# Gate and up projections of two SwiGLU blocks: another form of Strassen's seven products, with results made in place in PSUM

## The chip, the cores and the metric

The kernel runs on one core of a Trainium2 chip. The metric is the device time of one execution in microseconds (us). A core has five engines that run their own queues of instructions and wait for one another through semaphores: PE (TensorE, matrix products; its weight loads are shown as PEld), DVE (VectorE), ACT (ScalarE), POOL (GpSimd) and SP (SyncE, which issues most of the transfers). Matrix products write into PSUM, which has eight banks of 128 partitions by 512 float32 values; DVE and ACT can read and write it too.

## The reference, cut to what matters

One layer of a decoder, 1024 tokens of width 1024, in float32. A gated feed-forward block (SwiGLU, hidden width 2816) stands before and after a mixer of delta-rule and state-space heads:

```python
def swiglu(h, w_gate, w_up, w_down):
    a = jnp.einsum("bld,df->blf", h, w_gate)
    b = jnp.einsum("bld,df->blf", h, w_up)
    return jnp.einsum("blf,fd->bld", jax.nn.silu(a) * b, w_down)

x = x + 0.5 * swiglu(rms_norm(x, ffn1_norm[i]), ffn1_w_gate[i], ffn1_w_up[i], ffn1_w_down[i])
x = x + hybrid_mixer(rms_norm(x, mix_norm[i]), w_in[i], ...)
x = x + 0.5 * swiglu(rms_norm(x, ffn2_norm[i]), ffn2_w_gate[i], ffn2_w_up[i], ffn2_w_down[i])
```

## The kernel before

**Precision.** Each factor of a product is split into a high part, rounded to fp32r (ACT, the "cast" of L239), and the rest, also fp32r (DVE, L240). A product is three matrix products, high by high, high by low and low by high, added in one PSUM bank (L332, L333, L334 in `prod`).

**Strassen.** The gate and up projections are made by Strassen's form. The weights of one *item* are 256 columns of `w_gate` or of `w_up` and all 1024 rows: four blocks of 512 by 128, called a11, a12, a21, a22. The normalised and transposed tokens are four blocks of 512 by 512, two of them from the first 512 tokens (`x0`) and two from the last (`x1`). Seven products of sums of weight blocks by sums of token blocks, with sums of the products, give the four blocks c11, c12, c21, c22 of the result. A product is 12 matmuls (4 steps over the 512 rows, 3 parts each) of 512 columns; an item is 84 matmuls. There are 22 items in each feed-forward block (11 column groups, gate and up in turn): items 0 and 1 are written out, items 2 to 21 are a loop.

**Operands of the tokens.** `b_first` (L261) makes what needs only `x0`, `b_second` (L271) the rest: transposes on PE (L216, four of 128 by 128 into one bank with tag "sc"), scaling, sums and splits on ACT and DVE. This is done once in each block, before and while the first products run.

**Operands of the weights.** `a_load` brings an item's weights (1 MB) into one of two `wst` buffers. `a_ops` (L304) makes the sums (DVE, L315) and the splits for a group of up to four products, into one of two pairs of buffers `ah`, `al`. In the loop an item's next operands are made in two groups (`A_GROUPS`), called by `prep(0)` and `prep(1)`. `a_start` makes those of items 0 and 1 in the four groups of `A_START`.

**Results.** `open_bank` (L336) makes a product in a fresh bank and, where asked, copies it to SBUF (ACT, L341). In the loop products 3, 2 and 1 are copied so; 5, 4 and 7 are then added by PE to the same banks, 6 has the bank "oo". Six sums on DVE (L445, L446, L450, L451, L461, L464) put the four blocks together. For a gate item ACT takes the silu (L454, L455, L466, L467); for an up item DVE multiplies (L458, L459, L470, L471) and `hid_store` makes five sums (L490) and stores seven operands of the next product, the down projection, to DRAM.

**Order.** Each engine works through its own queue in order. The queues' orders are set when the program is built, by a planner that goes by the written order as priority and takes, at each point of its own estimate of time, the first instruction that it holds for ready. `tc.issue_after` adds an edge to that. A tile gets its buffer when the earlier tile of its tag is done with it. PSUM's banks have the tags "pj" (3), "mx" (2), "sc" (2) and "oo" (1).

**The stages in time.** Gate and up of the first block run from about 17 to 453 us, its down projection (L552 to L554) to about 667, the mixer with its input and output projections (L121 to L123) to 1657, gate and up of the second block to about 2088, its down projection to the end.

Of the kernel before, what the change touches and what calls it, by code (L numbers as in the profile page):

```python
# [21 lines left out]
P = 128  # L22
# [22 lines left out]
def kernel(  # L45
# [196 lines left out]
    def split(hi, lo, src):  # L242
# [7 lines left out]
    B_TAGS = {2: (ha, "h0", "h1"), 4: (ha, "h2", "h3"), 7: (ha, "h4", "h5"), 6: (ha, "h6", "h7"),  # L250
              3: (None, "b0", "b1"), 1: (None, "b2", "b3"), 5: (None, "b4", "b5")}
# [9 lines left out]
    def b_first(pool, x0, wcol, H, r11):  # L261

        for k in range(4):
            A.mul(out=r11[:, k], in_=transposed(x0, k), mul=wcol[:, k:k + 1])
            split(b_op(H, 2)[0][:, k], b_op(H, 2)[1][:, k], r11[:, k])
            t = pool.tile([P, 512], F32, name="bs4", tag="q")
            V.scalar_tensor_tensor(out=t, in0=transposed(x0, k + 4), scalar=wcol[:, k + 4:k + 5],
                                   in1=r11[:, k], op0=ALU.mult, op1=ALU.subtract)
            split(b_op(H, 4)[0][:, k], b_op(H, 4)[1][:, k], t)

    def b_second(pool, x0, x1, wcol, H, r11, r22, between):  # L271

        def operand(m, k, f):
            t = pool.tile([P, 512], F32, name="bs", tag="q")
            f(t)
            return split2(b_op(H, m)[0][:, k], b_op(H, m)[1][:, k], t)

        def scaled(pt, kx, other, op):
            return lambda t: V.scalar_tensor_tensor(out=t, in0=pt, scalar=wcol[:, kx:kx + 1], in1=other,
                                                    op0=ALU.mult, op1=op)  # L280

        for k in range(4):
            A.mul(out=r22[:, k], in_=transposed(x1, k + 4), mul=wcol[:, k + 4:k + 5])
            p12 = transposed(x1, k)
            operand(3, k, scaled(p12, k, r22[:, k], ALU.subtract))
            operand(6, k, scaled(p12, k, r11[:, k], ALU.add))
        between(0)
        for k in range(4):
            split(b_op(H, 5)[0][:, k], b_op(H, 5)[1][:, k], r22[:, k])
        for k in range(4):  # L290
            operand(7, k, scaled(transposed(x0, k + 4), k + 4, r22[:, k], ALU.add))
        between(1)
        for k in range(4):
            last = operand(1, k, lambda t: V.tensor_tensor(out=t, in0=r11[:, k], in1=r22[:, k], op=ALU.add))
        return last

    A_GROUPS = ((3, 2, 1, 5), (4, 7, 6))
# [6 lines left out]
    def a_ops(pool, *prods):  # L304

        hi = wp.tile([P, 4, 4, P], F32R, name="ah", tag="whi")
        lo = wp.tile([P, 4, 4, P], F32R, name="al", tag="wlo")
        for i, (raw, m, ops) in enumerate(prods):
            a11, a12 = raw[:, 0:4, 0:P], raw[:, 4:8, 0:P]
            a21, a22 = raw[:, 0:4, P:2 * P], raw[:, 4:8, P:2 * P]  # L310
            v = {3: a11, 4: a22, 2: (a21, a22, ALU.add), 1: (a11, a22, ALU.add), 5: (a11, a12, ALU.add),
                 7: (a12, a22, ALU.subtract), 6: (a21, a11, ALU.subtract)}[m]
            if isinstance(v, tuple):
                t = pool.tile([P, 4, P], F32, name="as", tag="q")
                V.tensor_tensor(out=t, in0=v[0], in1=v[1], op=v[2])  # L315
                v = t
# [5 lines left out]
    A_START = (((0, 2), (0, 4), (1, 2), (1, 4)), ((0, 3), (1, 3), (0, 6), (1, 6)),  # L322
               ((0, 5), (1, 5), (0, 7), (1, 7)), ((0, 1), (1, 1)))
# [4 lines left out]
    def prod(H, bank, ops, m, first):  # L328
# [6 lines left out]

    def open_bank(H, st, c, m, t, tag=None):  # L336

        bank = st[c] = psum(tag or {"c12": "pj", "c21": "mx", "c11": "pj", "c22": "oo"}[c])
        prod(H, bank, st, m, True)
        if t is not None:  # L340
            A.copy(out=t, in_=bank)  # L341
            st[f"m{m}"] = t

    def first_products(pool, H, ops):

        for st in ops:
            open_bank(H, st, "c21", 2, pool.tile([P, 512], F32, name="m2f"))
            prod(H, st["c21"], st, 4, False)
        for st in ops:
            open_bank(H, st, "c12", 3, pool.tile([P, 512], F32, name="m3", tag="q"))  # L350

    def gate_up_all(pool, H, w_gate, w_up, scr, raws, ops, last, work, tail):

        todo = [(p, w) for p in range(NF2) for w in (w_gate, w_up)]
        loads = todo[4:]

# [3 lines left out]
        def next_load():  # L360
            raws.pop(0)
            if loads:
                pn, wn = loads.pop(0)
                raws.append(a_load(wn, pn))


        for c, m in (("c22", 6), ("c11", 7)):
            for j, st in enumerate(ops):
                open_bank(H, st, c, m, wtile(True, f"m{m}"), ("pj", "oo")[j])
            if m == 6:  # L370
                for st in ops:
                    prod(H, st["c12"], st, 5, False)
        s12, s21 = (wtile(True, name) for name in ("sg12", "sg21"))
        nxt = [{}]

        def gated(o, bank, j):
            if j == 0:
                return A.activation(out=o, in_=bank, func=AF.Silu)
            return V.tensor_tensor(out=o, in0=bank, in1=o, op=ALU.mult)


        with tc.issue_after(last[0].ins), tc.issue_after(last[1].ins):
            for j, st in enumerate(ops):
# [1103 lines left out]
```

## Time and profile before

| | us |
|---|---|
| median of 3 runs | 2309.02 (2308.48 to 2310.09) |
| the profiled execution | 2309.97 |
| its span, first to last instruction | 2308.2 |
| PE busy | 2272.5 (98%) |
| DVE busy | 1725.1 (75%) |
| ACT busy | 1088.8 (47%) |
| TensorE clock granted, mean | 0.998 |

An engine's busy time is the time in which at least one of its instructions was in work. Instructions overlap in the engine's pipeline: a row's duration of one instruction is longer than the step from one to the next. A matmul's end is modelled, so PE's busy share says little of its rate; the step from one start to the next does.

### The profile page before, as it was taken

How to read it: one execution, taken by the hardware profiler on the slowest of the kernel's cores; microseconds unless marked ns; L12 is line 12 of the kernel's file. 1: busy time of each engine (PE TensorE's matmuls, PEld its weight loads, DVE VectorE, ACT ScalarE, POOL GpSimd, SP SyncE). 2: the span in 40 equal slices, each digit the busy share in tenths (PEclk: the TensorE clock that was granted, in tenths of full speed). 3: DMA queues.
4: the chain of work that ended last, by engine and by line, in shares of the span. 5: the costliest groups of instructions: out<-in, count | busy, mean ns of one | idle time of the engine just before them, and what ended most of it. 6: DMA issues, size and time to landing. Idle time of an engine off the chain costs nothing.

```text
span 2308.2 us, 31393 instructions
## 1 busy us (share of the span) xinstructions
PE 2272.5 (98%) x11750; PEld 1858.9 (81%) x11750; DVE 1725.1 (75%) x3349; ACT 1088.8 (47%) x1884; POOL 53.1 (2%) x125
## 2 busy tenths in 40 slices
PE   7999999999999999999999999999999999999998
PEld 5788888888878888878788888788778888888886
DVE  7977776767765675668777888878688777766787
ACT  7433333343367785863555555332543333334344
POOL 0000000000000100000000000000000000000000
PEclk9999999999999999999999999999999999999999
DMA  3333332573652332232333322335223333329446
GB/s 111 127 114 102 105 109 97 178 278 128 222 179 78 92 92 81 67 85 74 83 101 83 82 74 73 104 110 193 79 84 117 109 103 105 109 88 354 139 154 214
DMA packets 231438, 281.42 MB, mean 122 GB/s; under 512 B 57449, under 2 KB 164045, under 8 KB 230261
## 3 DMA queue, kind: packets, MB, share of 16 engines
q1 hardware_dynamic: 231028, 279.31, 37.5%
q8 instruction: 92, 1.51, 0.3%
q14 instruction: 62, 0.50, 0.1%
q0 software_dynamic: 256, 0.10, 0.0%
HBM read 211.59 MB, written 67.77 MB: 121 GB/s over the span
## 4 chain that ended last, share of the span: by engine, by line
PE 87%; DVE 6%; ACT 3%; DMA 2%; issue 1%; SPq 0%; POOL 0%; DVEq 0%; ACTq 0%
PE ps_pj L121 9%; PE ps_pj L123 9%; PE ps_pj L122 9%; PE ps_pj L334 6%; PE ps_pj L332 6%; PE ps_pj L333 6%; PE ps_mx L332 3%; PE ps_mx L334 3%; PE ps_mx L333 3%; PE ps_pj L553 2%; PE ps_pj L554 2%; PE ps_pj L552 2%; PE ps_oo L333 2%; PE ps_oo L332 2%; PE ps_oo L334 2%; PE ps_sc L552 1%
## 5 line engine op out<-in xcount | busy, mean ns | idle before, releaser
L121 PE MATMUL ps_pj<-hhi,whi 128*128 128x512 f32 x832 | 334.3, 402 | 0.4 <-ACT gsb L826 0.4
L123 PE MATMUL ps_pj<-hhi,wlo 128*128 128x512 f32 x832 | 334.5, 402 | 0.0
L122 PE MATMUL ps_pj<-hlo,whi 128*128 128x512 f32 x832 | 331.8, 399 | 0.0
L334 PE MATMUL ps_pj<-bh,al 128*128 128x512 f32 x688 | 267.9, 389 | 0.0
L333 PE MATMUL ps_pj<-bl,ah 128*128 128x512 f32 x688 | 267.8, 389 | 0.0
L332 PE MATMUL ps_pj<-bh,ah 128*128 128x512 f32 x688 | 267.6, 390 | 0.0
L123 PEld LDWEIGHTS ps_pj<-hhi,wlo 128*128 128x128 f32 x832 | 156.7, 188 | 29.6 <-issue 1.9
L122 PEld LDWEIGHTS ps_pj<-hlo,whi 128*128 128x128 f32 x832 | 156.7, 188 | 29.1 <-issue 1.2
L121 PEld LDWEIGHTS ps_pj<-hhi,whi 128*128 128x128 f32 x832 | 156.8, 188 | 28.8 <-ACT gsb L826 0.9
L239 ACT CAST ah<-wst 128x512 fp32r<-128x512 f32 x88 | 54.6, 623 | 223.8 <-PE ps_oo L333 131.4
L239 ACT CAST hid<-hraw 128x1024 fp32r<-128x1024 f32 (+1 forms) x84 | 82.3, 981 | 147.9 <-PE ps_oo L554 62.5
L333 PEld LDWEIGHTS ps_pj<-bl,ah 128*128 128x128 f32 x688 | 129.2, 188 | 26.8
L334 PEld LDWEIGHTS ps_pj<-bh,al 128*128 128x128 f32 x688 | 129.1, 188 | 26.7
L332 PEld LDWEIGHTS ps_pj<-bh,ah 128*128 128x128 f32 x688 | 128.9, 188 | 26.5
L315 DVE TENSOR_TENSOR as<-wst 128x512 f32<-128x512 f32 x220 | 144.8, 683 | 3.3 <-DMA wst<-in_ffn_w_up_dram 3.1
L240 DVE TENSOR_TENSOR al<-as,ah 128x512 fp32r<-128x512 f32 x220 | 140.9, 684 | 4.8 <-ACT ah L239 4.0
L332 PE MATMUL ps_mx<-bh,ah 128*128 128x512 f32 x352 | 138.3, 395 | 4.0 <-ACT m L341 1.4
L333 PE MATMUL ps_mx<-bl,ah 128*128 128x512 f32 x352 | 138.3, 393 | 0.5 <-DVE bl L240 0.5
L334 PE MATMUL ps_mx<-bh,al 128*128 128x512 f32 x352 | 137.7, 391 | 0.3 <-DVE al L240 0.3
L239 ACT CAST ah<-as 128x512 fp32r<-128x512 f32 x220 | 125.0, 618 | 22.6 <-DVE as L315 22.6
L240 DVE TENSOR_TENSOR hid<-hraw,hid 128x1024 fp32r<-128x1024 f32 (+1 forms) x84 | 95.0, 1131 | 34.8 <-ACT hid L239 34.3
L341 ACT COPY m<-ps_pj 128x512 f32<-128x512 f32 x88 | 51.6, 588 | 124.5 <-PE ps_pj L334 122.3
(448 smaller groups left out, 5085.0 us busy)
## 6 DMA issues: line engine op xcount, KB each, us to landing
hraw<-hid_scr SPq DMA_DIRECT2D x70, 512.0 KB, 3.9
hid_scr<-hs SPq DMA_DIRECT2D x110, 256.0 KB, 2.3
wst<-in_ffn_w_down_dram SPq DMA_DIRECT2D x50, 512.0 KB, 4.7
wst<-in_ffn_w_gate_dram SPq DMA_DIRECT2D x22, 1024.0 KB, 5.6
wst<-in_ffn_w_up_dram SPq DMA_DIRECT2D x22, 1024.0 KB, 5.4
wst<-in_w_in_dram SPq DMA_DIRECT2D x36, 512.0 KB, 4.8
hid_scr<-sg SPq DMA_DIRECT2D x44, 256.0 KB, 2.0
keep<-in_ffn_w_down_dram SPq DMA_DIRECT2D x20, 512.0 KB, 5.5
```

The source lines that it names most:

```text
L121: T.matmul(o, lhsT=wh, rhs=mh, start=first, stop=False)
L122: T.matmul(o, lhsT=wh, rhs=ml, start=False, stop=False)
L123: T.matmul(o, lhsT=wl, rhs=mh, start=False, stop=last)
L239: return (A.copy(out=hi, in_=src), V.tensor_tensor(out=lo, in0=src, in1=hi.bitcast(F32), op=ALU.subtract))
L240: V.tensor_tensor(out=lo, in0=src, in1=hi.bitcast(F32), op=ALU.subtract))
L315: V.tensor_tensor(out=t, in0=v[0], in1=v[1], op=v[2])
L332: T.matmul(bank, lhsT=wh[:, k], rhs=bh[:, k], start=a, stop=False, skip_group_check=True)
L333: T.matmul(bank, lhsT=wh[:, k], rhs=bl[:, k], start=False, stop=False, skip_group_check=True)
L334: T.matmul(bank, lhsT=wl[:, k], rhs=bh[:, k], start=False, stop=z, skip_group_check=True)
L341: A.copy(out=t, in_=bank)
L552: T.matmul(bank, lhsT=hh, rhs=wh, start=first and k == 0, stop=False, skip_group_check=True)
L553: T.matmul(bank, lhsT=hh, rhs=wl, start=False, stop=False, skip_group_check=True)
```

## The change

The seven products become those of the form with nested additions: with s1 = a21 + a22, s2 = s1 - a11, s3 = a21 - a11, s4 = a12 - s2 on the weights and four nested sums on the tokens, the seven products are numbered 1 (a11), 2 (a12), 3 (s4), 4 (a22), 5 (s1), 6 (s2), 7 (s3). Results grow in banks: product 6 goes into a bank y, product 1 (already made, and copied to SBUF as t1) is added to y **in place in PSUM** by DVE, the sum is copied out, PE adds product 7 to the same bank, DVE reads it, and PE adds product 4 to it. Product 1 of an item is made during the item before. An item has 4 sums on weights instead of 5, 3 sums on results instead of 6, 3 copies out of PSUM as before, and the same 84 matmuls. Items 0 and 1 are made product by product for both. `b_first` and `b_second` make the other token operands, with 16 groups of four transposes in a block instead of 20.

```diff
-    B_TAGS = {2: (ha, "h0", "h1"), 4: (ha, "h2", "h3"), 7: (ha, "h4", "h5"), 6: (ha, "h6", "h7"),
-              3: (None, "b0", "b1"), 1: (None, "b2", "b3"), 5: (None, "b4", "b5")}
+    B_TAGS = {1: (ha, "h0", "h1"), 2: (ha, "h2", "h3"), 3: (ha, "h4", "h5"), 4: (ha, "h6", "h7"),
+              6: (None, "b0", "b3"), 5: (None, "b1", "b4"), 7: (None, "b2", "b5")}
+    def b_first(x0, wcol, H, r11):
+        r21 = ha.tile([P, 4, 512], F32, name="r21", tag="h7")
+        for m, r, k0 in ((1, r11, 0), (2, r21, 4)):
+            for k in range(4):
+                hi, lo = (t[:, k] for t in b_op(H, m))
+                pt = transposed(x0, k + k0)
+                w = wcol[:, k + k0:k + k0 + 1]
+                A.mul(out=hi, in_=pt, mul=w)
+                V.scalar_tensor_tensor(out=lo, in0=pt, scalar=w, in1=hi.bitcast(F32),
+                                       op0=ALU.mult, op1=ALU.subtract)
+                A.mul(out=r[:, k], in_=pt, mul=w)
+        return r21
+    def b_second(pool, x1, wcol, H, r11, r21, r22, between):
+        def put(m, k, src):
+            return split2(b_op(H, m)[0][:, k], b_op(H, m)[1][:, k], src)
+        for k in range(4):
+            p12 = transposed(x1, k)
+            w = wcol[:, k:k + 1]
+            t1 = pool.tile([P, 512], F32, name="bs", tag="q")
+            V.scalar_tensor_tensor(out=t1, in0=p12, scalar=w, in1=r11[:, k], op0=ALU.mult, op1=ALU.subtract)
+            put(5, k, t1)
+            A.mul(out=r22[:, k], in_=transposed(x1, k + 4), mul=wcol[:, k + 4:k + 5])
+            t3 = pool.tile([P, 512], F32, name="bs", tag="q")
+            V.scalar_tensor_tensor(out=t3, in0=p12, scalar=w, in1=r22[:, k], op0=ALU.mult, op1=ALU.subtract)
+            put(7, k, t3)
+            V.tensor_tensor(out=r11[:, k], in0=r11[:, k], in1=t3, op=ALU.subtract)
+        between(0)
+        for k in range(4):
+            put(6, k, r11[:, k])
+        t4 = []
+        for k in range(4):
+            put(3, k, r22[:, k])
+            t4.append(pool.tile([P, 512], F32, name="bs", tag="q"))
+            V.tensor_tensor(out=t4[k], in0=r21[:, k], in1=r11[:, k], op=ALU.subtract)
+        between(1)
+        for k in range(4):
+            last = put(4, k, t4[k])
...
-    A_START = (((0, 2), (0, 4), (1, 2), (1, 4)), ((0, 3), (1, 3), (0, 6), (1, 6)),
-               ((0, 5), (1, 5), (0, 7), (1, 7)), ((0, 1), (1, 1)))
+    A_START = (((0, 1), (1, 1), (0, 2), (1, 2)), ((0, 5), (1, 5), (0, 7), (1, 7)),
+               ((0, 6), (1, 6), (0, 3), (1, 3)), ((0, 4), (1, 4)))
...
     def first_products(pool, H, ops):
         for st in ops:
+            st["x"] = prod(H, psum("pj"), st, 1, True)
+            st["t1"] = pool.tile([P, 512], F32, name="m1f")
+            A.copy(out=st["t1"], in_=st["x"])
         for st in ops:
+            prod(H, st["x"], st, 2)
...
+        for st, tag in zip(ops, ("pj", "oo")):
+            st["z"] = prod(H, psum(tag), st, 5, True)
         for st in ops:
+            st["w"] = prod(H, psum("mx"), st, 7, True)
+        for st in ops:
+            st["y"] = prod(H, psum("sc"), st, 6, True)
+        s11 = wtile(True, "s11")
+        silu(s11, ops[0]["x"])
+        for gate, st in zip((True, False), ops):
+            st["u"], st["r"] = wtile(gate, "u2"), wtile(gate, "r")
+            plus(st["u"], st["y"], st["t1"])
+            plus(st["w"], st["w"], st["u"])
+            A.copy(out=st["r"], in_=st["z"])
+            plus(st["r"], st["w"], st["r"])
+            prod(H, st["z"], st, 3)
+        ready((2, 1), (2, 5), (2, 6), (2, 2))
+        for st in ops:
+            prod(H, st["w"], st, 4)
...
+        for i in range(2, n):
+            p, gate, st = todo[i][0], i % 2 == 0, S[i]
+            y = prod(H, psum("mx"), st, 6, True)
+            z = prod(H, psum("sc"), st, 5, True)
+            c22 = wtile(gate, "r")
+            A.copy(out=c22, in_=z)
+            ready(*([(i, 7)] if i == 2 else []), *([(i + 1, 1)] if i + 1 < n else []), (i, 4), (i, 3))
+            next_load(i)
+            if i == 2:
+                first_hid()
+            plus(y, y, t1)
+            c12 = wtile(gate, "u2")
+            A.copy(out=c12, in_=y)
+            prod(H, x, st, 2)
...
+            prod(H, y, st, 7)
+            plus(c22, y, c22)
+            if i + 1 < n:
+                x1, t1 = first(i + 1)
+                ready((i + 1, 5), (i + 1, 6), (i + 1, 2), (i + 1, 7)) if i + 1 > 2 else None
+            else:
+                for f in tail:
+                    f()
+            prod(H, y, st, 4)
...
+            prod(H, z, st, 3)
+            plus(c12, c12, z)
```

`ready` calls `a_ops` for the named (item, product) pairs, `first(i)` makes product 1 of item i in a bank "pj" and copies it to `t1` (ACT), `plus` is one sum on DVE, `silu` one ACT instruction, `times` one DVE product. Where the lines are left out in the loop, the gate item takes its silus and the up item its products and `hid_store`, as before. The edges by `tc.issue_after` behind `b_second` are gone.

## Rows read from the trace of the kernel before

**Rows 1.** The page, first part: busy us of each engine (share) xinstructions.
```profile
PE 2272.5 (98%) x11750; PEld 1858.9 (81%) x11750; DVE 1725.1 (75%) x3349; ACT 1088.8 (47%) x1884; POOL 53.1 (2%) x125
```

**Rows 2.** Windows, inside the loop: stretch; PE, PEld, DVE, ACT, POOL busy; PEclk; DMA.
```profile
240.00:300.00 60.00, 60.00 (x266) 49.71 (x265) 41.98 (x69) 21.34 (x38) 0.00 (x0) 1.00 0.28 92
```

**Rows 3.** Timeline of PE in the loop and at its end: start, duration, instruction.
```profile
197.14 0.39 PE L332 MATMUL ps_mx<-bh,ah 128*128 128x512 f32 x1
...
199.86 0.39 PE L332 MATMUL ps_pj<-bh,ah 128*128 128x512 f32 x1
...
216.18 0.39 PE L332 MATMUL ps_mx<-bh,ah 128*128 128x512 f32 x1
...
452.59 0.39 PE L334 MATMUL ps_oo<-bh,al 128*128 128x512 f32 x1
452.82 0.39 PE L552 MATMUL ps_pj<-wd,hid 128*128 128x512 f32 x1
```

**Rows 4.** Timeline of PE at the first block's start; brackets: idle before, releaser.
```profile
23.62 1.04 PE L216 MATMUL ps_sc<-ident,xt 128*128 128x128 f32 x8
...
69.27 0.39 PE L332 MATMUL ps_pj<-bh,ah 128*128 128x512 f32 x1
...
72.99 0.50 PE L332 MATMUL ps_mx<-bh,ah 128*128 128x512 f32 x1 [0.84 <-ACT sg L378]
...
95.78 0.50 PE L332 MATMUL ps_mx<-bh,ah 128*128 128x512 f32 x1 [0.68 <-ACT m L341]
...
96.82 0.50 PE L334 MATMUL ps_mx<-bh,al 128*128 128x512 f32 x1 [0.30 <-DVE al L240]
```

**Rows 5.** Timeline of PE at the second block's start.
```profile
1691.26 0.39 PE L334 MATMUL ps_pj<-bh,al 128*128 128x512 f32 x1
1692.99 0.73 PE L332 MATMUL ps_sc<-bh,ah 128*128 128x512 f32 x2 [1.35 <-ACT bh L239]
...
1694.87 0.63 PE L334 MATMUL ps_sc<-bh,al 128*128 128x512 f32 x1
...
1706.34 0.39 PE L332 MATMUL ps_pj<-bh,ah 128*128 128x512 f32 x1
...
1731.65 0.50 PE L332 MATMUL ps_mx<-bh,ah 128*128 128x512 f32 x1 [0.68 <-ACT m L341]
```

**Rows 6.** Timeline of DVE in the loop.
```profile
200.78 0.68 DVE L315 TENSOR_TENSOR as<-wst 128x512 f32<-128x512 f32 x1
201.38 0.68 DVE L451 TENSOR_TENSOR m<-m,ps_pj 128x512 f32<-128x512 f32 x1
...
217.42 1.89 DVE L240 TENSOR_TENSOR al<-as,ah 128x512 fp32r<-128x512 f32 x3
219.22 0.68 DVE L450 TENSOR_TENSOR m<-ps_mx,m 128x512 f32<-128x512 f32 x1
```

**Rows 7.** Timeline of ACT in the loop.
```profile
203.50 0.63 ACT L466 ACTIVATE m<-m 128x512 f32<-128x512 f32 x1 [0.32 <-DVE m L461]
205.33 0.62 ACT L239 CAST ah<-wst 128x512 fp32r<-128x512 f32 x1 [1.19 <-PE ps_oo L333]
...
208.27 0.59 ACT L341 COPY m<-ps_pj 128x512 f32<-128x512 f32 x1 [0.75 <-PE ps_pj L334]
```

**Rows 8.** Timeline of DVE from the first `x1` operand to the first sum of results.
```profile
35.94 1.41 DVE L279 SCALAR_TENSOR_TENSOR bs<-ps_sc,cols,keepx 128x512 f32<-128x512 f32 x2 [2.03 <-ACT keepx L283]
...
67.40 0.68 DVE L385 TENSOR_TENSOR m<-m,m2f 128x512 f32<-128x512 f32 x1
...
1665.58 1.41 DVE L279 SCALAR_TENSOR_TENSOR bs<-ps_sc,cols,keepx 128x512 f32<-128x512 f32 x2 [2.12 <-ACT keepx L283]
...
1697.57 0.68 DVE L385 TENSOR_TENSOR m<-m,m2f 128x512 f32<-128x512 f32 x1
```

**Rows 9.** Windows at the two starts (columns as in rows 2).
```profile
22.00:26.00 4.00, 4.00 (x24) 3.08 (x22) 3.30 (x6) 4.00 (x8) 0.00 (x0) 1.00 0.00 0
...
1695.00:1700.00 5.00, 5.00 (x19) 3.95 (x18) 4.88 (x9) 2.19 (x4) 0.00 (x0) 0.75 0.53 174
```

More of the change, by code (lines that the diff above doesn't have):

```diff
@@ L271, in b_second @@
[L271 to L282, printed above, removed]
+    def b_first(x0, wcol, H, r11):
[10 more added lines that the diff above has]
+        return r21
@@ L334, in prod @@
             T.matmul(bank, lhsT=wl[:, k], rhs=bh[:, k], start=False, stop=z, skip_group_check=True)
[L336 to L342, printed above, removed]
+        return bank
     def first_products(pool, H, ops):
         for st in ops:
-            open_bank(H, st, "c21", 2, pool.tile([P, 512], F32, name="m2f"))
-            prod(H, st["c21"], st, 4, False)
+            st["x"] = prod(H, psum("pj"), st, 1, True)
+            st["t1"] = pool.tile([P, 512], F32, name="m1f")
+            A.copy(out=st["t1"], in_=st["x"])
@@ L349, in first_products, with gate_up_all @@
         for st in ops:
-            open_bank(H, st, "c12", 3, pool.tile([P, 512], F32, name="m3", tag="q"))
-    def gate_up_all(pool, H, w_gate, w_up, scr, raws, ops, last, work, tail):
+            prod(H, st["x"], st, 2)
+    def gate_up_all(pool, H, w_gate, w_up, scr, raws, ops, work, tail):
         todo = [(p, w) for p in range(NF2) for w in (w_gate, w_up)]
         loads = todo[4:]
+        raw = dict(zip((2, 3), raws))
+        S = {i: {} for i in range(2, len(todo))}
         def wtile(gate, name):
@@ L358, in wtile, with silu, times, plus @@
             return work.tile([P, 512], F32, name=name, tag="sg" if gate else "mu", bufs=8 if gate else 3)
-        def next_load():
-            raws.pop(0)
+        def silu(o, src):
+            A.activation(out=o, in_=src, func=AF.Silu)
+        def times(o, src):
+            V.tensor_tensor(out=o, in0=src, in1=o, op=ALU.mult)
+        def plus(o, x, y):
+            V.tensor_tensor(out=o, in0=x, in1=y, op=ALU.add)
+        def ready(*prods):
+            a_ops(pool, *((raw[j], m, S[j]) for j, m in prods))
@@ L362, in next_load @@
+        def next_load(i):
+            del raw[i]
             if loads:
                 pn, wn = loads.pop(0)
[L364 to L383, printed above, removed]
-                q, pp = st["m3"], st["m2"]
-                V.tensor_tensor(out=q, in0=q, in1=pp, op=ALU.subtract)
-                V.tensor_tensor(out=pp, in0=st["c21"], in1=q, op=ALU.add)
-                V.tensor_tensor(out=pp, in0=pp, in1=st["c12"], op=ALU.subtract)
-                if j == 0:
-                    gated(s12, st["c12"], 0)
-                    silu = gated(s21, st["c21"], 0)
-                    grp = a_ops(pool, *((raws[0], m, nxt[0]) for m in A_GROUPS[0]))
@@ new lines, in gate_up_all, with first @@
+        ready((2, 1), (2, 5), (2, 6), (2, 2))
+        for st in ops:
+            prod(H, st["w"], st, 4)
+        def first(i):
+            x = prod(H, psum("pj"), S[i], 1, True)
+            t = pool.tile([P, 512], F32, name="m1f")
+            A.copy(out=t, in_=x)
+            return x, t
+        x, t1 = first(2)
+        g, u = ops
+        s21 = wtile(True, "s21")
+        silu(s21, g["w"])
+        plus(g["u"], g["u"], g["z"])
+        silu(g["u"], g["u"])
+        silu(g["r"], g["r"])
@@ L472, in gate_up_all @@
+            prod(H, z, st, 3)
+            plus(c12, c12, z)
+            x = x1
+            if gate:
+                silu(c12, c12)
+                s12, s22 = c12, c22
+            else:
+                times(s12, c12)
                 hid_store(work, scr, p, s12, s22, s11, s21)
```

146 lines of the change are left out of this document (47 added, 99 removed).

## The prediction

> **What bounds the kernel now.** I read the page's busy shares first [rows 1], then the windows by stage, then PE's own timeline. The shares say PE 98%, DVE 75%, ACT 47%; as a matmul's busy time overlaps the next one's, the share alone can't say that PE is at its rate. The windows show it for the loop: all 60 us busy in a stretch of 60 us, with 266 matmuls [rows 2]. The timeline gives the step: an item goes from 197.14 to 216.18, so 19.04 us for 84 matmuls, 0.2267 us each, and 12 matmuls, one product, take 2.72 us (197.14 to 199.86) [rows 3]. By that step the 1368 starts from 130 to 440 us leave nothing over. So in the loop PE waits for nobody, and DVE, at 42 of 60 us, and ACT, at 21, lie beside it [rows 2]. The passage to the down projection has no gap either: 452.59 to 452.82 is one step [rows 3].
>
> What is not at that rate are the two starts. In the first block PE idles 0.84, 0.68 and 0.30 us ahead of 72.99, 95.78 and 96.82 [rows 4], which from start to start, less the step, is 0.99, 0.83 and 0.47 us lost; in the second it loses 1.5 us ahead of 1692.99 and 0.8 behind it, then runs at half rate until about 1697, and loses 0.83 ahead of 1731.65 [rows 5]. All excess of PE from 14 to 130 us is 10.9 us, and 7.4 from 1590 to 1800. That is all that a better order of results can win.
>
> **The loop, part by part.** Matmuls: 84 an item before and after, so PE's floor stays, 40 items of 19.04 us. Removed: one sum on weights and three on results, 4 DVE instructions an item; their step is 0.60 us (three in 1.89, of which the last lasts 0.68) [rows 6], 2.4 us an item, about 100 us of DVE in all. They lie beside PE, which waits for none of them, so they are worth nothing. ACT's three copies stay.
>
> Added are waits of PE. I count from an item's first matmul, with products at 0 (6), 2.72 (5), 5.44 (2), 8.16 (7), 10.88 (1 of the next item), 13.60 (4) and 16.32 (3); a result is there 0.16 us behind the last step (a matmul lasts 0.39 [rows 3]) and 0.09 passes to the next engine (a copy starts at 208.27 where the product's last matmul ends at 208.18 [rows 7]). First, product 7 waits for the sum in place and the copy out of it: 2.97 + 0.68 + 0.1 + 0.59 = 4.4 us against 8.16, 3.8 to spare. No row shows a DVE write to PSUM; the nearest are a sum that reads PSUM (0.68) and a split between SBUF tiles (the step of 0.60) [rows 6]. I take 0.68, and twice as much still fits. Second, product 4 waits for DVE's reading of the bank behind product 7: 11.13 + 0.68 + 0.1 = 11.9 against 13.60, 1.7 to spare, almost three DVE steps. Third, product 3 waits for a copy made ten us earlier. Behind a waiting matmul the whole PE queue stands, so these spares are what matters; DVE has 14 instructions in a gate item and 23 in an up item, 8.4 and 13.9 us of 19.04, and can keep them. Weight operands: the buffers of the group (5, 6, 2, 7) come free at 11.1 and are needed at 19.0; those of (1, 4, 3) come free at 0.2 and are needed from 10.9. Loads of 1 MB, one per item, keep their place. I cost the loop at nothing; if the cover of product 4 is lost, it is up to 1 us an item.
>
> The last item has no product 1 to cover product 4. The exposed chain would be 0.25 + 0.68 + 0.1 = 1.0 us, twice in the kernel; but product 3 is ready and the planner takes what is ready. I take 0, and 2 us for the upper end. The down projection's first operands use buffers free at product 7's end, 5 us ahead of their need: 0.
>
> **The starts.** Transposes: 16 fewer in a block; eight in a row last 1.04 us with the last one's end [rows 4], 0.1 us a step, so 1.6 us of PE. Before `x1` is there, DVE has 4 instructions fewer and ACT 4 more (0.58 us each, 2.3 us), and ACT is full at that time in the first block [rows 9]; `x1`'s statistics run on ACT too. I take 0 for the moment at which `x1` is ready, between -1 and +2.3 us in the first block, and 0 in the second, where ACT has time.
>
> From the first `x1` operand to the last operand of items 0 and 1 DVE is the bound. Before: 48 instructions (12 that read PSUM and scale, with a step of 0.66, two in 1.41 less the last one's 0.75; 36 of 0.60; 29.7 us by the steps) from 35.94 to 67.40 and from 1665.58 to 1697.57 [rows 8], so 31.5 and 32.0 us with 1.8 and 2.3 of idle. After: the loop over k 20, the group (6, 3) 10, splits of product 6 four, of 3 with the nested sum eight, the group (4) two, splits of 4 four, and then six sums on results that PE's last products wait for, because product 4 goes into the bank which DVE has to update and read first. In all 54 (8 of 0.66, 46 of 0.60, 33.0 us), with the same idle 34.8 and 35.3 us. So they end at 70.7 and 1700.9, product 4 of the gate item starts three instructions earlier, at 69.0 and 1699.2, and after two products of 2.72 item 2 begins with its product 1 at 74.5 and 1704.6.
>
> Before, item 2 begins at 69.27 and 1706.34 [rows 4, 5] and then loses 2.3 and 0.9 us, which fall away since DVE has 18 instructions less in items 0 to 4: by the same measure 71.6 and 1707.2. So the first block loses 2.9 us and the second wins 2.6, +0.3 in sum. The fewer transposes are in that already: PE is no longer the bound there.
>
> But PE then stands before product 4: by its own work it would be through with product 3 at about 66 and 1695.6, some 3 us earlier. An idle time of 1.35 us was followed by half rate (the step behind 1694.87 is 0.43 us, and that matmul lasts 0.63 for 0.39; the window's granted clock 0.75 is a mean of the two levels, 1.2 and 2.4 GHz) [rows 5, 9], which cost about 1.6 us; gaps of 0.7 to 0.8 us elsewhere were not [rows 4]. I take it once in the two blocks, +1.6, with 0 and +6.4 as ends (before products 6 and 4 in both).
>
> **Sum.** 0.3 + 1.6 = +1.9 us on the profiled execution's 2309.97 us (span 2308.2 and 1.8 around it), so 2311.9; the median of the runs lies 0.95 below it, which gives 2311.0. The bounds: transposes, idle and waits at their best -5, at their worst (`x1` late, four falls of the clock, exposed last items) +11.
>
> A rule is weighed here. The profile shows ACT's queue out of written order: the silu of L466 at 203.50 runs ahead of the casts of L239 at 205.33, which the program writes first and whose buffer was not free [rows 7]; DVE's sum of L315 at 200.78 runs ahead of L451, written before it [rows 6]. By the Trainium skill, "PSUM — Partial Sum Buffer", section "Engine vs sequencer instructions", the queues of ScalarE and VectorE are strict FIFO, so an instruction that waits holds all behind it. The trace bears that out only for the order that the planner chose, not for the order written; the rival that follows from the written order is the third below.
>
> **The rivals.** *DVE's chain ends earlier.* If the ten instructions of the group (6, 3) run before `x1` comes, 6 us leave the chain; PE is the bound again, gains 1.6 us by the transposes in each block and drops its old losses of about 3 and 5 us: 2309.0 - 11 = 2298. For it: DVE is busy for 3.3 of 4 us only at that time [rows 9], and half idle before `x1` in the second block. Against it: before, the group called at the same place was not taken ahead either. 13%.
>
> *Slower by the starts.* The same chain, with `x1` late by up to 2.3 us in the first block and half rate behind each long gap. It decides from a gap of about 1.35 us on, and ends 5 to 10 us later: 2314 to 2319, say 2316. For it: every gap of the chain that I find is longer than that. Against it: a fall hides in part behind DVE. 22%.
>
> *The loop waits.* If ACT and DVE kept the written order, ACT's copy of product 5 (5.7 us) and three casts with their splits would come before the sum in place: copy to 6.3, two casts to 7.3, sum and cast of product 3 to 9.5, its split to 10.3, sum in place to 10.9, copy to 11.6. Product 7 would start 3.5 us late in each of 40 items: +140, 2449 us. Against it are the two rows on the order. 5%.
>
> **How the numbers follow.** A measurement of this kernel tells 0.2%, 4.6 us, from no change. My forecast, within that, has 60%; of its spread a little falls on either side. Faster by more: 13%. Slower by more: 22 + 5 = 27%. The range reaches from 2303.5, half way to the first rival, to 2319, the second one's end; it leaves out the loop that waits and most of the first rival.
>
> **What would show it.** In the loop 19.04 us an item and no wait of PE; DVE's busy time down by some 120 us (160 instructions of the loop and about 20 of the starts, 0.68 each) to about 1605, PE's matmuls as many as before. At the starts: the first matmul of item 2 near 74.5 and 1705, the wait ahead of product 4 put down to DVE's sums, and the granted clock below 1 in that stretch. Wrong would be: any wait at products 7 or 4 inside the loop, a period other than 19.04, or operands of product 3 and 6 made before `x1`.

## The result, and the profile after the change

The changed kernel takes 2314.7 us (median of 16 runs, 2311.65 to 2318.94), the kernel before 2309.88 beside it (16 runs): ratio 1.0023, interval 1.0015 to 1.0031. So it is slower by 4.8 us. The time lies inside the range, 3.7 us above the forecast, and just over the bound of 0.2% that was set for "no change": it has the size of the second rival. The profiled run took 2317.82 us, 3.1 above its median; where it is dearer than other runs is shown below.

The page of the changed kernel, part 1 (against [rows 1] DVE lost 108 us, and PE has 32 transposes fewer), and windows in the loop [rows 2] and at the two starts:

```profile
PE 2271.4 (98%) x11718; PEld 1859.5 (80%) x11718; DVE 1617.3 (70%) x3169; ACT 1088.0 (47%) x1884; POOL 53.2 (2%) x125
...
240.00:300.00 60.00, 60.00 (x266) 49.71 (x265) 33.07 (x53) 21.46 (x40) 0.00 (x0) 1.00 0.30 100
...
63.70:67.40 3.70, 3.66 (x9) 2.86 (x10) 3.70 (x8) 0.47 (x1) 0.00 (x0) 0.56 0.83 256
...
1702.60:1706.00 3.40, 3.40 (x8) 2.72 (x9) 3.40 (x7) 0.44 (x1) 0.00 (x0) 0.50 0.94 302
```

Each window shows start:end and length, then the busy time of PE, PEld, DVE, ACT and POOL, the granted clock and the DMA's share. In the loop nothing has changed for PE, 266 matmuls in 60 us, and DVE is 8.9 us lighter. At the starts PE had 0.56 and 0.50 of its clock. PE's timeline shows why (start, duration, instruction, and in brackets the idle time before and what ended it; in order: a period of the loop, the start of block 1, of block 2, and the last item of block 1):

```profile
250.43 0.39 PE L353 MATMUL ps_mx<-bh,ah 128*128 128x512 f32 x1
...
269.47 0.39 PE L353 MATMUL ps_mx<-bh,ah 128*128 128x512 f32 x1
...
60.57 0.39 PE L355 MATMUL ps_sc<-bh,al 128*128 128x512 f32 x1
63.74 0.50 PE L353 MATMUL ps_pj<-bh,ah 128*128 128x512 f32 x1 [2.77 <-ACT r L407]
...
67.41 0.48 PE L353 MATMUL ps_pj<-bh,ah 128*128 128x512 f32 x1
...
70.91 0.39 PE L353 MATMUL ps_mx<-bh,ah 128*128 128x512 f32 x1
...
76.35 0.39 PE L353 MATMUL ps_pj<-bh,ah 128*128 128x512 f32 x1
...
1702.60 0.80 PE L353 MATMUL ps_pj<-bh,ah 128*128 128x512 f32 x1 [3.03 <-ACT r L407]
...
1715.20 0.39 PE L353 MATMUL ps_pj<-bh,ah 128*128 128x512 f32 x1
...
453.95 0.50 PE L353 MATMUL ps_mx<-bh,ah 128*128 128x512 f32 x1 [1.18 <-DVE r L384]
```

An item takes 269.47 - 250.43 = 19.04 us, as in [rows 3]. In both starts PE stands for about 3 us ahead of product 3 (bank "pj" at 63.74 and 1702.60), not ahead of product 4, and it waits for ACT, not for DVE. Behind it nine matmuls take 67.41 - 63.74 = 3.67 us in place of 2.04: half rate (steps of 0.43 us), the lower level of 1.2 GHz, 1.6 us lost in each block. Product 4 (70.91) then begins without a wait, and item 2 at 76.35 and 1715.20 (before, at 69.27 and 1706.34 [rows 4, 5]).

What ACT did instead, and DVE's chain at the same time (block 1):

```profile
58.97 0.62 ACT L239 CAST bh<-bs 128x512 fp32r<-128x512 f32 x1 [2.77 <-DVE bs L298]
...
62.58 0.62 ACT L239 CAST bh<-bs 128x512 fp32r<-128x512 f32 x1 [0.59 <-DVE bs L298]
63.11 0.58 ACT L407 COPY r<-ps_pj 128x512 f32<-128x512 f32 x1
...
34.19 0.75 DVE L284 SCALAR_TENSOR_TENSOR bs<-ps_sc,cols,keepx 128x512 f32<-128x512 f32 x1 [0.96 <-PE ps_sc L216]
...
63.67 2.49 DVE L240 TENSOR_TENSOR bl<-bs,bh 128x512 fp32r<-128x512 f32 x4
...
68.47 1.28 DVE L384 TENSOR_TENSOR r<-ps_mx,r 128x512 f32<-128x512 f32 x2
```

Product 5 was through at about 50, but its copy (L407), which product 3 needs before it adds to the same bank, stands in ACT's queue behind the four casts of product 4's token operand, and each of these waits for a sum of DVE's chain. DVE's sums for product 4 (L384) end at 69.7, the gate item's at 69.2. So copy and sums come due within 6 us of each other, and both behind the same chain. Beyond DVE's chain the late copy and the half rate cost about 1.8 us in block 1 (69.15 to 70.91) and 2.2 in block 2 (1707.5 to 1709.76): without them product 4 would have waited for DVE until then.

There is a third stretch of low clock, earlier in block 1, with a granted clock of 0.51 to 0.76 in every kernel that has the new form there (window, then a transpose of PE and an instruction of DVE; the kernel before has 1.00 of the clock there):

```profile
30.00:37.00 7.00, 4.22 (x14) 3.11 (x15) 5.30 (x10) 6.77 (x11) 0.00 (x0) 0.51 0.00 0
...
32.43 0.69 PE L216 MATMUL ps_sc<-ident,xt 128*128 128x128 f32 x2 [2.57 <-ACT xt L186]
...
38.09 0.75 DVE L284 SCALAR_TENSOR_TENSOR bs<-ps_sc,cols,keepx 128x512 f32<-128x512 f32 x1 [1.11 <-PE ps_sc L216]
```

PE waits there for ACT, runs transposes and matmuls at the lower level, and DVE's chain waits 1.11 us for one of these transposes. In all DVE idles 2.3 us within the chain of block 1, and 0.3 in block 2.

From profiled run to profiled run the kernel gained 7.85 us. By the last matmul of each stage: gate and up 1 ends at 458.39 for 452.59 (+5.80), down 1 takes 217.68 for 214.74 (+2.94), up to the last projection +1.04 (not followed), gate and up 2 -1.62, down 2 -0.29.

### The profile page after: what moved, and what is told of

Its sections match the earlier page's. It is cut to its first block, busy times and chain, and to the rows that moved or that the text cites. A ratio compares the mean times of both kernels' runs of the same rounds, so it can differ in the third digit from the quotient of the medians.

```text
span 2316.1 us, 31014 instructions
## 1 busy us (share of the span) xinstructions
PE 2271.4 (98%) x11718; PEld 1859.5 (80%) x11718; DVE 1617.3 (70%) x3169; ACT 1088.0 (47%) x1884; POOL 53.2 (2%) x125
## 4 chain that ended last, share of the span: by engine, by line
PE 85%; DVE 7%; ACT 4%; DMA 2%; issue 1%; SPq 0%; POOL 0%; DVEq 0%; ACTq 0%
PE ps_pj L121 9%; PE ps_pj L123 9%; PE ps_pj L122 9%; PE ps_mx L353 5%; PE ps_mx L354 5%; PE ps_mx L355 5%; PE ps_pj L353 3%; PE ps_pj L354 3%; PE ps_pj L355 3%; PE ps_sc L354 3%; PE ps_sc L355 3%; PE ps_sc L353 3%; PE ps_pj L560 2%; PE ps_pj L559 2%; PE ps_pj L561 2%
## 5 line engine op out<-in xcount | busy, mean ns | idle before, releaser
L353 PE MATMUL ps_mx<-bh,ah 128*128 128x512 f32 x512 | 199.4, 389 | 1.2 <-DVE r L384 1.2
L355 PE MATMUL ps_mx<-bh,al 128*128 128x512 f32 x512 | 199.2, 389 | 0.0
L353 PE MATMUL ps_pj<-bh,ah 128*128 128x512 f32 x368 | 146.8, 400 | 6.4 <-ACT r L407 5.8
L354 PE MATMUL ps_pj<-bl,ah 128*128 128x512 f32 x368 | 145.8, 396 | 0.0
L355 PE MATMUL ps_pj<-bh,al 128*128 128x512 f32 x368 | 145.6, 396 | 0.0
L354 PE MATMUL ps_sc<-bl,ah 128*128 128x512 f32 x336 | 130.6, 390 | 0.0
L353 PE MATMUL ps_sc<-bh,ah 128*128 128x512 f32 x336 | 130.4, 389 | 0.0
L355 PE MATMUL ps_sc<-bh,al 128*128 128x512 f32 x336 | 130.4, 389 | 0.0
L353 PEld LDWEIGHTS ps_mx<-bh,ah 128*128 128x128 f32 x512 | 96.1, 188 | 21.9 <-DVE r L384 2.0
L355 PEld LDWEIGHTS ps_mx<-bh,al 128*128 128x128 f32 x512 | 96.1, 188 | 20.1
```

The source lines that it names most:

```text
L353: T.matmul(bank, lhsT=wh[:, k], rhs=bh[:, k], start=a, stop=False, skip_group_check=True)
L354: T.matmul(bank, lhsT=wh[:, k], rhs=bl[:, k], start=False, stop=False, skip_group_check=True)
L355: T.matmul(bank, lhsT=wl[:, k], rhs=bh[:, k], start=False, stop=z, skip_group_check=True)
```

## The experiments

Theory A: DVE's chain of 54 instructions bounds the start, and the copy stands only in front of it. Theory B: ACT's late copy and the half rate behind it are the cause. Theory C: part of the loss comes from what the planner makes of stages that the change does not touch. Beside each time stands the ratio to the kernel before, run on the same chip. As the loads at the very start land up to 2 us apart from run to run, the starts are compared by the time from DVE's first operand of `x1` to product 6 of item 2, which is 44.9 us in block 1 of the changed kernel and 43.3 in block 2.

**The copies first.**

```diff
-        for k in range(4):
-            last = put(4, k, t4[k])
-        return last
+        H["rest"] = lambda: [put(4, k, t4[k]) for k in range(4)]
...
+            st["r"] = wtile(gate, "r")
+            made.append(A.copy(out=st["r"], in_=st["z"]))
+        with tc.issue_after(made[0].ins), tc.issue_after(made[1].ins):
+            H["rest"]()
...
```

> The two copies of product 5 out of its bank are written ahead of the four casts of product 4's token operand, and those casts queue behind them on ACT; nothing is left out. In the changed kernel product 3 waits for these copies to 63.74 us in block 1 and runs at half rate to 67.4; item 2 begins at 76.35. Theory A (DVE's chain of 54 instructions is the bound, the late copy stands only in front of it): product 3 begins at 60.6 without a wait, product 4 then waits some 2 us for DVE's third sum, which ends at about 67.9 as now; item 2 at 73.5, or 74.5 to 75 with a fall of the clock behind that wait; 1.4 to 2.9 us a block, 2309 to 2312 us. Theory B (ACT's copy is the cause, with the half rate behind it): product 4 follows product 3 at 66.0 without a wait, item 2 at 71.5, 4.9 us a block, about 2305 us.

2315.36 us, 1.0026 (1.0016 to 1.0036): nothing gained, and neither theory's number came. The copies ran at 49.3 and 52.7, and product 3 did start without a wait. Then the planner had put product 1 of item 2 ahead of product 4, and PE stood there (timelines of PE, ACT, SP and DVE):

```profile
71.43 0.50 PE L351 MATMUL ps_pj<-bh,ah 128*128 128x512 f32 x1 [2.77 <-ACT ah L239]
...
70.76 1.14 ACT L239 CAST ah<-wst 128x512 fp32r<-128x512 f32 x2 [5.33 <-DMA wst<-in_ffn_w_gate_dram]
...
65.40 0.38 SPq L304 DMA_DIRECT2D wst<-in_ffn_w_gate_dram  x1
...
70.70 1.27 DVE L382 TENSOR_TENSOR r<-ps_mx,r 128x512 f32<-128x512 f32 x2
```

The cast waits for item 2's weights. Their load is issued at 65.40, when DVE has split product 4's weights and so freed the buffer, and lands at about 70.7. A third condition thus comes due in the same few us, and it hangs on DVE's chain too. Product 4 could not have begun before either: the gate item's sum for it ends at about 71.4. So A's wait came, at product 1 in place of product 4, with half rate behind it. The time from `x1` to item 2's product 6 was 46.2 us in block 1 and 42.8 in block 2, for 44.9 and 43.3.

**Four DVE instructions fewer behind the casts.**

```diff
+            if m == 4:
+                H[m] = b_op(H, m)[0], H[6][1]
+                return A.copy(out=H[m][0][:, k], in_=src)
```

Product 4 then reads the low part of product 6's token operand, in every item of the block.

> Left out: the low part of product 4's token operand (four DVE instructions a block; the product takes product 6's low part in its place). The copies stay where the changed kernel has them. Theory A (DVE's chain alone sets the end): the chain is 4 x 0.60 = 2.4 us shorter, item 2 begins at about 74.0 in block 1, 2310 us. Theory B: product 3 still waits for the copy to 63.7 and runs at half rate, item 2 stays at 76.3 and the time at 2314.7.

2324.38 us, 1.0062 (1.0047 to 1.0077). The start is as B says: product 3 still waits 2.77 us for the copy (at 64.93), and `x1` to product 6 takes 45.4 and 43.4 us, no gain. The 9.7 us more lie elsewhere, at the seams to the down projections. Down 1 takes 221.0 us and down 2 215.3, some 7 and 4 more than in kernels whose seams do not wait (the last matmul of product 4, SP's issue of a load, ACT's cast of it and PE's first matmul of down 1):

```profile
456.50 0.39 PE L358 MATMUL ps_mx<-bh,al 128*128 128x512 f32 x1
...
456.69 0.32 SPq L539 DMA_DIRECT2D hraw<-hid_scr  x1
...
461.78 1.04 ACT L239 CAST hid<-hraw 128x1024 fp32r<-128x1024 f32 x1 [3.73 <-DMA hraw<-hid_scr]
...
462.88 0.79 PE L562 MATMUL ps_pj<-wd,hid 128*128 128x512 f32 x1 [4.17 <-ACT hid L239]
```

This is the edit's own doing. Product 6's low part has the tag "b3" (`B_TAGS` in the diff), and the down projection's first `hraw` load goes into the buffer of that tag. As product 4 now reads that part, the buffer stays taken until product 4 of the last item is through, and the load is issued 0.2 us behind it.

**Both.** The two edits together.

> Both edits: the copies first, and the low part of product 4's token operand left out. Theory A: with 2.4 us off DVE's chain the wait ahead of product 4 that the copies alone leave goes too, item 2 begins at 71.5 in block 1, 2 us a block or more below the copies alone, about 2305 us. Theory B: as with the copies alone, since DVE is not late; within 0.5 us a block of that run.

2316.09 us, 1.0026 (1.0015 to 1.0037). At the start A holds: 42.4 and 40.3 us, 3.8 and 2.5 less than with the copies alone, where A expected 2 or more and B none; what is left is a short wait for DVE. In the time it does not show, because the seam waits again (PE; then the load of `hraw` into that buffer in the changed kernel; then here):

```profile
69.49 0.47 PE L354 MATMUL ps_mx<-bh,ah 128*128 128x512 f32 x1 [0.46 <-DVE r L385]
...
458.70 0.71 PE L565 MATMUL ps_pj<-wd,hid 128*128 128x512 f32 x1 [2.26 <-ACT hid L239]
```
```profile
443.61 0.42 SPq L536 DMA_DIRECT2D hraw<-hid_scr  x1
```
```profile
454.43 0.32 SPq L542 DMA_DIRECT2D hraw<-hid_scr  x1
```

In the changed kernel the load goes when product 6 of the last item is through (its last matmul starts at 443.32); here it goes 10.8 us later, when product 4 is (454.24). Half rate follows the wait, and block 2 has the same. Down 1 takes 217.7 us for about 214, down 2 215.7 for about 211; without that the run would have taken some 2308 us (an estimate: 2316.1 less 3.7 and 4.8), near A's 2305. Theory C is not needed for these two runs.

**Product 3 first in the last item.**

```diff
+            if i + 1 == n:
+                prod(H, z, st, 3)
             prod(H, y, st, 4)
...
-            prod(H, z, st, 3)
+            if i + 1 < n:
+                prod(H, z, st, 3)
```

> In the last item of each block product 3 is written before product 4. My step took for granted that the planner does so itself. If the exposed chain is all there is: the wait of 1.18 us ahead of product 4 at 453.95 goes, the gate and up part of block 1 ends 1.2 to 1.3 us earlier, nothing in block 2 (0.12 there), in all about 2313.5 us, to be read in the trace and not in the time. Rival: product 4's results then come last and the last stored sums later, so the down projection begins with a wait of the same size and the time stays.

2312.11 us, 1.0008 (0.9999 to 1.0018), 2.6 less than the changed kernel. The wait is gone, product 4 follows product 3 within a step and the down projection follows at once:

```profile
454.85 0.39 PE L355 MATMUL ps_sc<-bh,al 128*128 128x512 f32 x1
455.08 0.39 PE L353 MATMUL ps_mx<-bh,ah 128*128 128x512 f32 x1
...
457.80 0.39 PE L562 MATMUL ps_pj<-wd,hid 128*128 128x512 f32 x1
```

That accounts for 1.3 us; the other 1.3 of the medians I can't place.

**The new form in one block only.** The other block keeps the functions of the kernel before.

> The new form in block 2 alone, block 1 as before. Theory S (the cost lies in block 1's start and in what the planner makes of the stages behind it): gate and up 1 ends at 452.6, down 1 at 667.3 and the projections as before; only block 2's start changes, by -1.8 us as in the changed kernel: 2308 us, 0.1% below before. Rival T (the loss belongs to the new form wherever it stands, half and half): about +2.4 us, 2312.

> The new form in block 1 alone, block 2 as before. Theory S: gate and up 1 +5.8, down 1 +2.9, projections and mixer +1.0 (if that comes from block 1) or 0 (if it comes from block 2's operands being made beside the mixer's end), so +8.7 to +9.7 us, 2318.6 to 2319.6, slower than the whole change. Rival T: about +2.4 us, 2312.

Block 2 alone: 2308.29 us, 0.9991 (0.9982 to 1.0001), 1.6 below the kernel before. Block 1 alone: 2315.16, 1.0022 (1.0013 to 1.0032), 5.3 above. Theory S holds for where the cost lies: gate and up 1 ends at 458.25, +5.7. It fails for down 1, which takes 213.82 us here and 217.68 in the profiled run of the changed kernel, though up to block 2 both run the same instructions in the same order. The difference is a load, not the planner (the same sum of DVE and then the same matmul of PE; each fence first the changed kernel, then block 1 alone):

```profile
637.88 1.23 DVE L538 TENSOR_TENSOR wst<-wst 128x1024 f32<-128x1024 f32 x1 [2.95 <-DMA wst<-in_ffn_w_down_dram]
...
650.75 1.19 PE L216 MATMUL ps_sc<-ident,xtb 128*128 128x128 f32 x4 [2.47 <-ACT xtb L186]
```
```profile
635.43 1.23 DVE L538 TENSOR_TENSOR wst<-wst 128x1024 f32<-128x1024 f32 x1 [1.91 <-DMA wst<-in_ffn_w_down_dram]
...
648.31 0.94 PE L216 MATMUL ps_sc<-ident,xtb 128*128 128x128 f32 x4 [0.18 <-ACT xtb L186]
```

In the changed kernel's run the sum waits 1.0 us longer for its weights, and the one two places ahead of it had waited 1.75 for 0.32. That delays ACT's scaling of `x`, and PE has no cover there: it waits 2.3 us more, and half rate follows (from 652 to 654 us a granted clock of 0.50 for 1.00), another 1.6 us. Down 1 took 213.6 to 214.9 us in eight of the other kernels and 214.74 before. So the +2.94 belongs to that run.

**The casts of down 1 behind the scaling.** They were made to queue behind L186 by `tc.issue_after`.

> In the changed kernel the down projection's casts that come after ACT's scaling of the first half of x (the two of 1.1 us at 649.55) are made to queue behind it; the changed kernel has three of them ahead of it, before has two. Theory C (the planner's order in a stage that the change does not touch costs 2.9 us there): the wait of 2.47 us at 650.75 goes, down 1 takes 214.7 us or less in place of 217.7; -2.9 us, 2311.8. Rival: the matmuls of the down projection then wait for their own casts, and down 1 stays at 216 to 218.

2318.43 us, 1.004 (1.0025 to 1.0055). The wait is halved and not gone:

```profile
650.41 0.66 PE L218 MATMUL ps_sc<-ident,xtb 128*128 128x128 f32 x4 [1.33 <-ACT xtb L188]
```

Down 1 takes 215.44 us, and behind it waits of 1.37 and 1.12 us for ACT, 0.30 and 0.38 in the changed kernel, stand in the first projections. That is between the two expectations, 214.7 or less and 216 to 218, so neither came. With the run of block 1 alone, theory C is out for this stage, and no run shows it elsewhere.

**Four more sums ahead of product 4 in the loop**, and product 3 held behind it:

```diff
+            for op in (ALU.add, ALU.subtract) * 2:
+                V.tensor_tensor(out=c22, in0=c22, in1=y, op=op)
             plus(c22, y, c22)
...
-            prod(H, z, st, 3)
+            with tc.issue_after(ended[0].ins):
+                prod(H, z, st, 3)
```

> The cover of product 4 in the loop, by itself: four more sums on DVE (plus and minus the same bank, so the result stays) between the end of product 7 and product 4, and product 3 held behind product 4. The spare counted for product 4 was 1.7 us; four sums are 2.4 us. If spare and step hold: a wait of 0.7 us ahead of product 4 in each of 40 items, 19.7 us an item, about 2314.7 + 28 = 2343 us, and the clock stays at its upper level behind so short a gap. If the spare was larger than counted (3 us): no wait and 2315. If each gap makes the clock fall: over 1 us more an item, 2380 or more.

One run, 2323.47 us; no other shows how it scatters. In the loop PE does not wait at all:

```profile
240.00:300.00 60.00, 60.00 (x266) 49.69 (x266) 42.09 (x68) 21.23 (x38) 0.00 (x0) 1.00 0.36 118
```

The planner had put product 6 of the next item ahead of product 4. So the spare of 1.7 us that I counted is right as a time (in the changed kernel DVE's reading ends at 243.2 and product 4 starts at 244.99), but in this run it is no limit: the cover that was used up was filled from what was ready. The 8.8 us lie outside the loop; the waits at the two seams (2.0 and 0.9 us in block 1, as much in block 2) are the larger part that I found, the rest was not followed.

**The sums on POOL.** With the first three runs a theory D: copy, sums and load hang on one chain, and only what shortens it ahead of all three helps. The six sums of the start's group (6, 3) go to POOL.

```diff
-    a_ops(pool, *((raws[j], m, ops[j]) for j, m in A_START[n]))
+    a_ops(pool, *((raws[j], m, ops[j]) for j, m in A_START[n]), summer=G if n == 2 else V)
...
```

> The six sums on weights of the start's group for products 6 and 3 go from DVE to POOL, in both blocks; nothing is left out. After the runs with the copies first (no gain, product 1 of item 2 then waited for the load of item 2's weights) and without the low part alone (no gain either, product 3 kept waiting for the copy), theory D: the copy, DVE's sums and the load of item 2's weights all hang on the same DVE chain and come due within 3 us of each other, so only what shortens the chain ahead of all three helps. These six stand ahead of all three: 6 x 0.60 = 3.6 us. The copy comes at about 60, product 3 begins at 60.6 in place of 63.7 with no half rate behind it, item 2 at 72 to 73 in place of 76.35; 3.6 us a block or a little more, 2307 to 2308 us. Rival: POOL is slow with two operands (no row of it in this kernel; its nearest is a select on 128x1024, 1.4 to 1.7 us, so 0.7 to 0.9 for half the columns) or holds DVE up, and product 6 waits for its weights: no gain, 2314 to 2317.

> The six sums on POOL, and product 3 ahead of product 4 in the last item of each block, which alone brought 2.6 us (1.2 of them by the wait at the last item). If the two add up: 2307.5 - 2 = 2305.5 us, 0.2% below the kernel before. If the order at the seam to the down projection changes with it: up to 4 us more.

> As the one with the sums on POOL and the last item's order, and with the copies of product 5 ahead of product 4's casts. Theory D: with the chain 3.6 us shorter the copy is no longer last, so its place is worth nothing or up to 1 us a block: 2304 to 2306 us. If the copy was a bound of its own: 2 us a block below the run without it.

2316.15, 2313.34 and 2314.25 us; ratios 1.0028 (1.0018 to 1.0037), 1.0019 (1.001 to 1.0028) and 1.0025 (1.0014 to 1.0036). The rival came: no gain in any of them. DVE and then POOL in the second run:

```profile
47.37 0.74 DVE L288 SCALAR_TENSOR_TENSOR bs<-ps_sc,cols,keepx 128x512 f32<-128x512 f32 x1
...
49.08 1.77 DVE L290 TENSOR_TENSOR keepx<-keepx,bs 128x512 f32<-128x512 f32 x1
50.78 1.78 DVE L240 TENSOR_TENSOR bl<-bs,bh 128x512 fp32r<-128x512 f32 x1
52.70 5.79 DVE L240 TENSOR_TENSOR al<-as,ah 128x512 fp32r<-128x512 f32 x4
...
45.73 4.58 POOL L320 TENSOR_TENSOR as<-wst 128x512 f32<-128x512 f32 x2 [39.70 <-DVE bl L240]
50.27 3.44 POOL L330 TENSOR_TENSOR as<-as,wst 128x512 f32<-128x512 f32 x2
```

While POOL makes its sums, most of them at 1.74 us each, DVE's instructions on two SBUF tiles last 1.77 us in place of 0.68; the one that reads PSUM and one SBUF tile, at 47.37, keeps its 0.74. DVE gave up six instructions and lost about as much on the others: `x1` to product 6 took 45.2 us in block 1 of the second run. A test of theory D this was not, since the chain did not get shorter.

**The sums ahead of `x1`.** In place in the loaded weights, two fewer, and written with the group (5, 7); product 3 first in the last item.

```diff
+            if start and m == 7:
+                v = a21
+                V.tensor_tensor(out=v, in0=a21, in1=a11, op=ALU.subtract)
...
+            if start and m == 7:
+                V.tensor_tensor(out=a21, in0=a21, in1=a22, op=ALU.add)
+                V.tensor_tensor(out=a12, in0=a12, in1=a21, op=ALU.subtract)
...
```

> Nothing is left out. The start's sums on weights are made in place in the loaded weights, two fewer a block, and are written with the group (5, 7), so that the planner puts them ahead of x1; product 3 ahead of product 4 in the last item. This makes by hand what the first rival of the prediction supposed, a chain behind x1 that lacks the sums of the group (6, 3): 54 - 6 = 48 instructions. Theory D (copy, sums and load all hang on that chain): 3.6 us earlier in block 2, where DVE is half idle before x1; in block 1 1.2 to 3.6, since four more instructions (2.4 us) stand ahead of DVE's scaling of x1. Product 3 waits for the copy 0 to 1 us in place of 3. Against the run with the last item's order alone (2312.1) 4.8 to 7.2 us less: 2305 to 2307.5 us, at or below the kernel before. If x1 comes later by as much as the chain gets shorter: 2311 to 2313. If the start is bound elsewhere by now: no gain in block 2 either, 2312.

2302.84 us (8 runs, 2301.1 to 2303.58), 0.9971 (0.996 to 0.9981): 9.3 less than with the last item's order alone (8.5 by the ratios), and 6.6 below the kernel before; 4.8 to 7.2 had been expected. Windows in block 2 and early in block 1, then PE, ACT and DVE in block 1:

```profile
1684.00:1704.00 20.00, 20.00 (x90) 16.57 (x89) 20.00 (x35) 10.92 (x20) 0.00 (x0) 1.00 0.34 106
...
30.00:37.00 7.00, 6.40 (x26) 5.07 (x27) 5.54 (x12) 5.73 (x10) 0.00 (x0) 0.76 0.01 4
...
60.73 0.50 PE L361 MATMUL ps_pj<-bh,ah 128*128 128x512 f32 x1 [1.65 <-ACT r L415]
...
60.09 0.58 ACT L415 COPY r<-ps_pj 128x512 f32<-128x512 f32 x1
...
65.46 1.28 DVE L392 TENSOR_TENSOR r<-ps_mx,r 128x512 f32<-128x512 f32 x2
```

In block 2 PE no longer stands at all between 1684 and 1704, at full clock. In block 1 the copy comes at 60.09 in place of 63.11, the wait is 1.65 us and no half rate follows it. `x1` to item 2's product 6 takes 38.2 us in both blocks, 6.6 and 5.1 less than in the changed kernel; against that, DVE's first operand of `x1` comes at 36.34 in block 1, 33.7 to 35.8 in the others. That is more than the six instructions, 3.6 us, because the half rate behind product 3's wait (1.6 us) goes too; the 1.4 us that block 1 has beyond that fit the idle time within DVE's chain, 0.7 us for 2.3, in part that of the early stretch, where the clock is 0.76 for 0.51. The copies kept their place behind the casts in this kernel. Theory D gave the right way, but this run does not part it from A, which asks for a gain from a shorter chain too. What speaks for D is that at the start the copies alone gained next to nothing, the four instructions behind the casts alone nothing either, and both together 2.5 and 3.0 us (44.9 and 43.3 to 42.4 and 40.3).

## Why the prediction was right, and where it was not

- **The loop: right.** 19.04 us an item and no wait. The reason was right too: DVE and ACT lay beside PE. DVE's busy time fell to 1617, not 1605: the count of 180 instructions was right, and each was worth its step, 0.60, not its duration, 0.68 (180 x 0.60 = 108). That the spare of 1.7 us is what matters was too strict, as far as the one run with four more sums shows.
- **DVE's chain: right.** 54 instructions, from 34.19 to 69.7 us: 35.5, for 34.8 counted; 33.5 in block 2, for 35.3. The low clock of block 1 from 30 us on, which reaches into its chain, was not foreseen.
- **The place of the wait: wrong.** "PE then stands before product 4" and "the wait ahead of product 4 put down to DVE's sums". I had put the copy of product 5 at no cost because in the loop it is made ten us early. At the start ACT's queue holds it behind four casts that wait for DVE. By the Trainium skill, "PSUM — Partial Sum Buffer", section "Engine vs sequencer instructions", the queues of ScalarE and VectorE are strict FIFO, so an instruction that waits holds all that is queued behind it. The trace agrees, for the order that the planner chose: the copy at 63.11. I had weighed this rule for the loop and not asked it of the start.
- **The size of the start: 1.1 us short.** Item 2 begins at 76.35, against 74.5 predicted, and at 1715.20 less the 9.78 by which the stage before ended later, 1705.4, against 1704.6. Against the kernel before that is +4.75 and -1.8, +2.95 in sum, for +0.3 and +1.6 for the clock. The clock fell in both blocks, not in one, and the 1.6 us counted in full in each: at full rate product 4 would have followed product 3 at 69.3 and 1708.1, just behind DVE's sums at 69.15 and 1707.5. With the wait for the copy that makes about 4.0 us beyond DVE's chain, for the 1.6 in the sum. That the start is only 1.1 short is partly luck: in block 2 the chain was 1.8 us shorter than counted and made up for much of it.
- **The last item: wrong.** "Product 3 is ready and the planner takes what is ready", 0 us. It took four matmuls of it, then product 4, which waited: 1.3 us in block 1 and 0.1 in block 2, inside the bound of 2.
- **The sum.** Predicted +1.9, measured +4.8: +1.3 for the last item, +1.1 for the start, and about 0.5 that the medians leave over and that I can't place between the loads of the stages behind.
- **The rivals.** *Slower by the starts* came in size, 2314.7 for 2314 to 2319, by half rate in both blocks; its other half, a late `x1`, did not. *DVE's chain ends earlier* did not happen by itself, but made by hand it gave 2302.8, for 2298 counted. *The loop waits* did not. "It decides from a gap of about 1.35 us on" did not hold: the length of a gap alone does not decide, as the last section shows.

## What to carry to other kernels

Where several engines hand a start to one another, list all the conditions of each product, with the queue that each stands in, before pricing one: here a copy, a sum and a load came due within a few us behind one chain, and taking one away showed only the next, while six instructions off the chain's head moved all three. A gap behind which the clock falls costs more than its length, so closing it can give back more than was cut. Compare stage by stage: where a far stage gets slower, look first for a buffer that the edit holds longer, as product 6's low part was held here, before blaming the planner. And compare several runs, since loads land differently.

## What the runs showed of the hardware that was not expected

- A DVE sum of two SBUF tiles lasts 1.77 us beside POOL's sums, 0.68 alone; the one DVE instruction there that reads PSUM and one SBUF tile did not slow down (0.74). By the Trainium skill, "SBUF — State Buffer", section "SBUF: two separate sides", a DVE instruction with two SBUF inputs and a POOL instruction that reads SBUF lock each other out of a shared pair of ports for a whole instruction. The trace agrees: steps of 1.7 us, the length of one POOL sum.
- The length of an idle time does not tell whether the granted clock falls behind it. It fell behind 2.77 and 3.03 us (nine matmuls, most at 0.43 us a step) and, in [rows 5], behind 1.35; it did not behind 1.18 (453.95), 1.65 (60.73, the last kernel), 2.33 or 3.04. The last two are waits for the same copy, with the sums on POOL and the last item's order (block 1), and with the casts of down 1 behind the scaling (block 2):

```profile
66.30 0.50 PE L353 MATMUL ps_pj<-bh,ah 128*128 128x512 f32 x1 [2.33 <-ACT r L407]
66.64 0.39 PE L354 MATMUL ps_pj<-bl,ah 128*128 128x512 f32 x1
```
```profile
1703.72 0.50 PE L355 MATMUL ps_pj<-bh,ah 128*128 128x512 f32 x1 [3.04 <-ACT r L409]
1704.05 0.39 PE L356 MATMUL ps_pj<-bl,ah 128*128 128x512 f32 x1
```

  What decides is not shown by these runs.
- Two DVE sums written in place into PSUM take 1.28 us, with the step of 0.60 of sums between SBUF tiles; the prediction had taken 0.68 for one.
